# Four 32-bit transposes between the matmuls, and one transfer queue in a fixed order, in a matmul with bias and residual

## The chip, the cores and the metric

The kernel runs on one core of a Trainium2 chip. The time is device microseconds of one execution, and the median of the runs is compared. Profiles are taken of one execution by the hardware profiler; their rows are in microseconds unless marked ns. PE is TensorE's matmul, PEld its weight load, DVE is VectorE, ACT ScalarE, POOL GpSimd and SP SyncE; a q behind a name is the engine's instruction queue, from which transfers are issued.

## The reference

```python
batch, m, k, n = 16, 512, 1024, 768
x: [16, 512, 1024] f32, weight: [1024, 768] f32, bias: [768] f32, residual: [16, 512, 768] f32

def reference(x, weight, bias, residual):
    return (np.matmul(x, weight) + bias + residual).astype(np.float32)
```

## The kernel before

x is taken as 8192 rows of 1024. A tile t is 128 of these rows, so there are 64 tiles; one matmul contracts 128 of the 1024 elements of a row, so a tile has eight steps k. In DRAM the rows are cut so that each of the 128 partitions holds neighbouring rows: four rows of x in one load (16 KB in a run, `stage_xload`, L156), two rows of the residual in one load (6 KB, `stage_resload`, L163) and two rows of the result in one store (L221).

A tile goes through four stages. `stage_a` casts its rows of x to bfloat16 on ScalarE (L94). `stage_b` transposes them on TensorE, eight times 128 x 128 of bfloat16, into the PSUM tile `psum_t` (L181), and VectorE copies `psum_t` to `xt_tile` in one instruction (L96). `stage_c` does sixteen matmuls (L197): for each k, one over 512 and one over 256 of the 768 columns, with the weights of `xt_tile` held in the array and the matrix `w_sb` streamed through it. `stage_d` adds the residual to the sum on VectorE (L217), and after every second tile ScalarE's queue issues the store. The bias is added to the residual ahead of that by GpSimd (L106, a helper's line, as L94 and L96 are).

The loop over t is written so that the transposes of tile t+1 come before the matmuls of tile t, and the addition of tile t-1 after them. Its order is the program's; the framework may move an instruction where its priorities say so, and sets the waits. Loads are issued from SP's queue, as are half the weights; the other half of the weights (`W_SPLIT_ACT`), the bias and all stores are issued from ScalarE's. At most eight transfers are in flight: the issue of one waits for the end of an earlier one, on one of eight semaphores.

At the start x, the weights in single steps of k and the residual are loaded; ScalarE and VectorE cast four steps of the weights each.

The buffers: 3 of x (four tiles each), 6 of the residual, 8 of the result, 4 of cast rows, 5 of `xt_tile`, 2 of `psum_t` and 3 of the matmul's sum `psum_o`.

Of the kernel before, what the change touches and what calls it, by code (L numbers as in the profile page):

```python
# [9 lines left out]

MM_DT = mybir.dt.bfloat16
XROWS = 4
RES_ROWS = 2
STORE_ROWS = 2
X_SWDGE = False
BIAS_ENGINE = "gpsimd"
WCV_SYNC_ENGINE = "scalar"
WCV_ACT_ENGINE = "vector"
CONVERT_ENGINE = "scalar"  # L20
COPYBACK_ENGINE = "vector"
PIPE_AB = 2
XB_BUFS = 4
X_BUFS = 3
RES_BUFS = 6
OUT_BUFS = 8
XT_BUFS = 5
POUT_BUFS = 3
PTRANS_BUFS = 2
W_SPLIT_ACT = 4  # L30
K_ROTATE = 4
# [3 lines left out]
def kernel(  # L35
# [9 lines left out]
    P = 128  # L45
    FP32 = mybir.dt.float32
    BF16 = mybir.dt.bfloat16

# [4 lines left out]
    Kw, N = weight.shape  # L53
    assert Kw == K
    n_k = K // P
    n_sub = M // P
    n_xload = M // (XROWS * P)
    n_resload = M // (RES_ROWS * P)
    RES_PER_X = XROWS // RES_ROWS

    x_ld = x2d.rearrange("(S p j) k -> S p j k", p=P, j=XROWS)
    res_4d = res2d.rearrange("(S p j) n -> S p j n", p=P, j=XROWS)
    out_4d = out2d.rearrange("(S p j) n -> S p j n", p=P, j=XROWS)

    def res_ld_ap(q):
        S, h = divmod(q, RES_PER_X)
        return res_4d[S, :, h * RES_ROWS:(h + 1) * RES_ROWS, :]

    def out_st_ap(sg):
        S, h = divmod(sg, XROWS // STORE_ROWS)  # L70
        return out_4d[S, :, h * STORE_ROWS:(h + 1) * STORE_ROWS, :]

    if N <= 512:
        n_chunks = [(0, N)]
    else:
        n_chunks = [(0, 512), (512, N - 512)]

    k_order = [(K_ROTATE + i) % n_k for i in range(n_k)]

    const = ctx.enter_context(tc.tile_pool(name="const", bufs=1))  # L80
    xin_pool = ctx.enter_context(tc.tile_pool(name="xin", bufs=1))
    xbf_pool = ctx.enter_context(tc.tile_pool(name="xbf", bufs=1))
    xt_pool = ctx.enter_context(tc.tile_pool(name="xt", bufs=1))
    res_pool = ctx.enter_context(tc.tile_pool(name="res", bufs=1))
    out_pool = ctx.enter_context(tc.tile_pool(name="outp", bufs=1))
    ptrans_pool = ctx.enter_context(tc.tile_pool(name="ptrans", bufs=1, space=bass.MemoryType.PSUM))
    pout_pool = ctx.enter_context(tc.tile_pool(name="pout", bufs=1, space=bass.MemoryType.PSUM))

    def rr_tile(pool, base, idx, nbufs, shape, dtype):
        return pool.tile(shape, dtype, name=base, tag=f"{base}{idx % nbufs}", bufs=1)  # L90

    def eng_copy(eng_name, out_ap, in_ap):
        if eng_name == "scalar":
            nc.scalar.copy(out=out_ap, in_=in_ap)  # L94
        elif eng_name == "vector":
            nc.vector.tensor_copy(out=out_ap, in_=in_ap)  # L96
        elif eng_name == "gpsimd":
            nc.gpsimd.tensor_copy(out=out_ap, in_=in_ap)
        else:
            nc.any.tensor_copy(out=out_ap, in_=in_ap)  # L100

    def eng_add(eng_name, out_ap, in0, in1):
        if eng_name == "vector":
            nc.vector.tensor_add(out=out_ap, in0=in0, in1=in1)
        else:
            nc.gpsimd.tensor_add(out=out_ap, in0=in0, in1=in1)  # L106

    warm = const.tile([1, 2], FP32, name="warm")
    nc.vector.memset(warm, 0.0)  # L109
    nc.scalar.copy(out=warm, in_=warm)  # L110

    ident = const.tile([P, P], BF16, name="ident")
    make_identity(nc, ident)

    w_dram = weight.rearrange("(ko ki) n -> ki ko n", ki=P)
    w_sb = const.tile([P, n_k, N], MM_DT, name="w_sb")
    w_stage = const.tile([P, n_k, N], FP32, name="w_stage")

    with tc.high_priority():
        bias_row = const.tile([1, N], FP32, name="bias_row")  # L120
        nc.scalar.dma_start(out=bias_row, in_=bias[None, :])
        for k in range(W_SPLIT_ACT):
            nc.scalar.dma_start(out=w_stage[:, k, :], in_=w_dram[:, k, :])

    ones_col = const.tile([1, P], BF16, name="ones_col")
    nc.vector.memset(ones_col, 1.0)  # L126
    bias_row16 = const.tile([1, N], BF16, name="bias_row16")
    nc.vector.tensor_copy(out=bias_row16, in_=bias_row)  # L128
    bias_psum = pout_pool.tile([P, N], FP32, name="bias_psum", tag="psum_o0", bufs=1)
    for (n0, nl) in n_chunks:  # L130
        nc.tensor.matmul(  # L131
            bias_psum[:, n0:n0 + nl],
            lhsT=ones_col,
            rhs=bias_row16[:, n0:n0 + nl],
            start=True,
            stop=True,
        )
    bias_bcast = const.tile([P, N], FP32, name="bias_bcast")
    nc.vector.tensor_copy(out=bias_bcast, in_=bias_psum)  # L139

    x_tiles = {}
    res_tiles = {}
    out_tiles = {}
    xb_tiles = {}
    xt_tiles = {}
    psum_o_tiles = {}

    def stage_xload(sx):
        if sx >= n_xload:
            return  # L150
        if X_SWDGE:
            x_tile = rr_tile(xin_pool, "x_tile", sx, X_BUFS, [P, XROWS, K], BF16)
            nc.gpsimd.dma_start(out=x_tile, in_=x_ld[sx])
        else:
            x_tile = rr_tile(xin_pool, "x_tile", sx, X_BUFS, [P, XROWS, K], FP32)
            nc.sync.dma_start(out=x_tile, in_=x_ld[sx])  # L156
        x_tiles[sx] = x_tile

    def stage_resload(q):
        if q >= n_resload:  # L160
            return
        res_tile = rr_tile(res_pool, "res_tile", q, RES_BUFS, [P, RES_ROWS, N], FP32)
        nc.sync.dma_start(out=res_tile, in_=res_ld_ap(q))  # L163
        res_tiles[q] = res_tile
        for j in range(RES_ROWS):
            eng_add(BIAS_ENGINE, res_tile[:, j, :], res_tile[:, j, :], bias_bcast)

    def stage_a(t):
        if t < 0 or t >= n_sub:
            return  # L170
        xb_tile = rr_tile(xbf_pool, "xb_tile", t, XB_BUFS, [P, K], BF16)
        eng_copy(CONVERT_ENGINE, xb_tile, x_tiles[t // XROWS][:, t % XROWS, :])
        xb_tiles[t] = xb_tile

    def stage_b(t):
        if t < 0 or t >= n_sub:
            return
        xin = xb_tiles.pop(t)
        psum_t = rr_tile(ptrans_pool, "psum_t", t, PTRANS_BUFS, [P, n_k, P], BF16)
        for k in range(n_k):  # L180
            nc.tensor.transpose(  # L181
                out=psum_t[:, k, :],
                in_=xin[:, ts(k, P)],
                identity=ident,
            )
        xt_tile = rr_tile(xt_pool, "xt_tile", t, XT_BUFS, [P, n_k, P], MM_DT)
        eng_copy(COPYBACK_ENGINE, xt_tile, psum_t)
        xt_tiles[t] = xt_tile

    def stage_c(t):  # L190
        if t < 0 or t >= n_sub:
            return
        xt_tile = xt_tiles.pop(t)
        psum_o = rr_tile(pout_pool, "psum_o", t, POUT_BUFS, [P, N], FP32)
        for i, k in enumerate(k_order):
            for (n0, nl) in n_chunks:
                nc.tensor.matmul(  # L197
                    psum_o[:, n0:n0 + nl],
                    lhsT=xt_tile[:, k, :],
                    rhs=w_sb[:, k, n0:n0 + nl],  # L200
                    start=(i == 0),
                    stop=(i == n_k - 1),
                )
        psum_o_tiles[t] = psum_o

    def stage_d(t):
        if t < 0 or t >= n_sub:
            return
        psum_o = psum_o_tiles.pop(t)
        res_tile = res_tiles[t // RES_ROWS]  # L210
        s2, j2 = divmod(t, STORE_ROWS)
        if j2 == 0:
            out_tiles[s2] = rr_tile(
                out_pool, "out_tile", s2, OUT_BUFS, [P, STORE_ROWS, N], FP32
            )
        out_tile = out_tiles[s2]
        nc.vector.tensor_add(  # L217
            out=out_tile[:, j2, :], in0=psum_o, in1=res_tile[:, t % RES_ROWS, :]
        )
        if j2 == STORE_ROWS - 1:  # L220
            nc.scalar.dma_start(out=out_st_ap(s2), in_=out_tiles.pop(s2))  # L221
        if t % RES_ROWS == RES_ROWS - 1:
            res_tiles.pop(t // RES_ROWS)

    next_xload = [0]
    next_res = [0]

    def ensure_xloaded(sx):
        while next_xload[0] <= min(sx, n_xload - 1):
            stage_xload(next_xload[0])  # L230
            next_xload[0] += 1

    def ensure_resloaded(q):
        while next_res[0] <= min(q, n_resload - 1):
            stage_resload(next_res[0])
            next_res[0] += 1

    ensure_xloaded(0)
    for k in range(W_SPLIT_ACT, n_k):
        nc.sync.dma_start(out=w_stage[:, k, :], in_=w_dram[:, k, :])  # L240
# [47 lines left out]
```

## Time and profile before

| what | value |
|---|---|
| time, median of 3 runs | 221.37 us (221.13 to 221.74) |
| span of the profiled execution | 219.0 us |
| median of the runs less that span | 2.4 us |
| TensorE busy, matmuls and transposes | 197.0 us (90%) |
| VectorE, ScalarE, GpSimd busy | 103.5, 68.3, 114.6 us |
| bytes moved, and mean rate | 87.29 MB, 399 GB/s |
| granted TensorE clock, mean | 0.998 |

The span runs from the first to the last instruction of the profiled execution. The page does not give a time of that execution on the outside, so the difference to the median of the runs stands in the table. "Busy" for TensorE includes the modelled ends of its matmuls. In a row of the timeline the first number is the start, the second the duration from the first start to the last end of the instructions merged into it; what stands in square brackets is how long the engine had been idle, and who ended that.

### The profile page before, as it was taken

Reading aid. Unit: us, or ns where it says so; the run is one execution under the profiler, and the core shown is the slowest. Engines: PE = TensorE matmul, PEld = TensorE weight load, DVE = VectorE, ACT = ScalarE, POOL = GpSimd, SP = SyncE. Lnnn points to the kernel's source line nnn. Section 1 sums busy time; section 2 is a strip of 40 time slices with the busy share of each in tenths; the row PEclk is TensorE's granted clock in tenths of the full one; section 3 lists DMA queues with packets and bytes.
Section 4 is the critical chain, followed back from the end, with each engine's and each line's share of the span. In section 5 each row is a group of like instructions: output and inputs, shape, how many; then the busy total and the mean of one; then the engine's idle time right before and its main releaser. Section 6 shows DMA issues by size and latency. Waiting matters only on the chain.

```text
span 219.0 us, 3761 instructions
## 1 busy us (share of the span) xinstructions
PE 197.0 (90%) x1509; PEld 130.3 (60%) x1538; DVE 103.5 (47%) x136; ACT 68.3 (31%) x70; POOL 114.6 (52%) x70
## 2 busy tenths in 40 slices
PE   1119989999999999999999999999999999999990
PEld 0115656666666666666666666666666666666660
DVE  1133454455544555445554455444554445544441
ACT  2362243352240706051420607051331607042000
POOL 1006751919275573909284663919184482918900
PEclk9999999999999999999999999999999999999999
DMA  7999999999999999999999999999999999999433
GB/s 235 399 409 440 428 404 441 413 424 439 412 436 412 434 413 433 428 422 430 419 435 416 441 409 435 428 420 432 413 434 414 444 405 436 427 413 398 188 144 144
DMA packets 12692, 87.29 MB, mean 399 GB/s; under 512 B 1409, under 2 KB 1409, under 8 KB 10626
## 3 DMA queue, kind: packets, MB, share of 16 engines
q1 hardware_dynamic: 7488, 60.30, 65.7%
q10 hardware_dynamic: 5186, 26.74, 29.5%
q8 instruction: 12, 0.20, 0.4%
q14 instruction: 6, 0.05, 0.1%
HBM read 61.87 MB, written 25.17 MB: 397 GB/s over the span
## 4 chain that ended last, share of the span: by engine, by line
PE 82%; issue 1%; DVE 0%; DVEq 0%
PE psum_o L197 71%; PE psum_t L181 12%; DVE out_tile L217 0%; DVEq L217 0%
## 5 line engine op out<-in xcount | busy, mean ns | idle before, releaser
L197 PE MATMUL psum_o<-w_sb,xt_tile 128*128 128x256 bf16 (+1 forms) x995 | 175.5, 326 | 7.5 <-DVE xt_tile L96 6.0
L106 POOL TENSOR_TENSOR res_tile<-res_tile,bias_bcast 128x768 f32<-128x768 f32 x64 | 113.9, 1813 | 93.1 <-DMA res_tile<-in_residual_dram 87.5
L197 PEld LDWEIGHTS <-xt_tile 128*128 128x128 bf16 x1024 | 97.8, 98 | 65.0 <-DVE xt_tile L96 6.2
L217 DVE TENSOR_TENSOR out_tile<-psum_o,res_tile 128x768 f32<-128x768 f32 x64 | 61.3, 957 | 96.7 <-PE psum_o L197 51.0
L94 ACT CAST xb_tile<-x_tile 128x1024 bf16<-128x1024 f32 x64 | 63.7, 1042 | 124.8 <-DMA x_tile<-in_x_dram 69.4
L181 PE MATMUL psum_t<-ident,xb_tile 128*128 128x128 bf16 x512 | 40.1, 223 | 6.5 <-ACT xb_tile L94 6.5
L96 DVE COPY xt_tile<-psum_t 128x1024 bf16<-128x1024 bf16 x64 | 43.4, 680 | 2.2 <-PE psum_t L181 2.2
L181 PEld LDWEIGHTS <-xb_tile 128*128 128x128 bf16 x512 | 34.8, 100 | 15.4 <-ACT xb_tile L94 7.3
L96 DVE CAST w_sb<-w_stage 128x768 bf16<-128x768 f32 x4 | 2.2, 560 | 10.5 <-DMA w_stage<-in_weight_dram 10.5
L94 ACT CAST w_sb<-w_stage 128x768 bf16<-128x768 f32 x4 | 3.3, 832 | 1.9 <-DMA w_stage<-in_weight_dram 1.9
L131 PE MATMUL bias_psum<-bias_row_97,ones_col 1*128 1x512 bf16 (+1 forms) x2 | 0.8, 498 | 2.7 <-DVE bias_row_97 L128 2.7
L110 ACT ACT_TABLE_LOAD x1 | 1.3, 1283 | 3.5 <-issue 3.5
L131 PEld LDWEIGHTS <-ones_col 1*128 1x128 bf16 x2 | 0.2, 99 | 2.6 <-issue 1.6
L128 DVE CAST bias_row_97<-bias_row 1x768 bf16<-1x768 f32 x1 | 0.5, 547 | 1.1 <-DMA bias_row<-in_bias_dram 1.1
L139 DVE COPY bias_bcast<-bias_psum 128x768 f32<-128x768 f32 x1 | 0.9, 950 | 0.0
L109 DVE MEMSET warm<- 1x2 f32 x1 | 0.1, 60 | 0.8 <-PEq L272 0.8
masks.py:197 POOL MEMSET ident<- 128x128 bf16 x1 | 0.2, 205 | 0.3 <-POOLq L272 0.3
masks.py:199 POOL TENSOR_SCALAR_AFFINE_SELECT ident<-ident 128x128 bf16<-128x128 bf16 x1 | 0.3, 293 | 0.1
L272 POOL MEMSET const-float32-0.0<- 128x1 f32 x1 | 0.1, 99 | 0.2 <-issue 0.2
L110 ACT COPY warm<-warm 1x2 f32<-1x2 f32 x1 | 0.2, 191 | 0.0
L126 DVE MEMSET ones_col<- 1x128 bf16 x1 | 0.2, 165 | 0.0
L272 POOL MEMSET const-bfloat16-1.0<- 128x1 bf16 x1 | 0.1, 103 | 0.0
(2 smaller groups left out, 0.2 us busy)
## 6 DMA issues: line engine op xcount, KB each, us to landing
x_tile<-in_x_dram SPq DMA_DIRECT2D x16, 2048.0 KB, 21.1
res_tile<-in_residual_dram SPq DMA_DIRECT2D x32, 768.0 KB, 19.1
out_dram<-out_tile ACTq DMA_DIRECT2D x32, 768.0 KB, 10.7
w_stage<-in_weight_dram SPq DMA_DIRECT2D x4, 384.0 KB, 9.7
w_stage<-in_weight_dram ACTq DMA_DIRECT2D x4, 384.0 KB, 10.9
bias_row<-in_bias_dram ACTq DMA_DIRECT2D x1, 3.0 KB
```

Of the source, the lines that this page charges most:

```text
L94: nc.scalar.copy(out=out_ap, in_=in_ap)
L96: nc.vector.tensor_copy(out=out_ap, in_=in_ap)
L106: nc.gpsimd.tensor_add(out=out_ap, in0=in0, in1=in1)
L110: nc.scalar.copy(out=warm, in_=warm)
L126: nc.vector.memset(ones_col, 1.0)
L128: nc.vector.tensor_copy(out=bias_row16, in_=bias_row)
L131: nc.tensor.matmul(bias_psum[:, n0:n0 + nl], lhsT=ones_col, rhs=bias_row16[:, n0:n0 + nl], start=True, stop=True,)
L139: nc.vector.tensor_copy(out=bias_bcast, in_=bias_psum)
L181: nc.tensor.transpose(out=psum_t[:, k, :], in_=xin[:, ts(k, P)], identity=ident,)
L197: nc.tensor.matmul(psum_o[:, n0:n0 + nl], lhsT=xt_tile[:, k, :], rhs=w_sb[:, k, n0:n0 + nl], start=(i == 0), stop=(i == n_k - 1),)
L217: nc.vector.tensor_add(out=out_tile[:, j2, :], in0=psum_o, in1=res_tile[:, t % RES_ROWS, :])
L272: nc = _bacc.Bacc("TRN2", target_bir_lowering=False, num_devices=1)
```

## The change

The kernel is written anew around the same arithmetic. In short:

- A row of x is still cast to bfloat16 on ScalarE, but it is transposed as 512 words of 32 bits, each of two neighbours. A tile takes four transposes in place of eight (`transpose`). A transposed word has two steps of the contraction in it, so the matmul takes every second element of `xt` as weights (`lhsT=xt_tiles[t][:, c, :, r]`), and the weight matrix is loaded with its rows paired in the same way (`w_dram`).
- The four transposes of tile t+1 stand between the matmuls of tile t, one behind the 512-wide matmul of k = 0, 2, 4 and 6. The copy out of PSUM remains one instruction for each tile.
- All transfers but the bias are issued from SP's queue in a written order, and the framework keeps the program's order on each engine (`tc.keep_in_program_order`). The residual is loaded, and the result stored, four rows to a partition (12 KB in a run). The last group is stored row by row. The first group of x is loaded row by row, between the weights.
- The first three tiles advance together through the steps of k as the weights come. All weights are cast on VectorE. 24 matmuls on the identity run on TensorE ahead of them, and the bias is broadcast by a matmul of float32.
- The result of the first three groups of four tiles is made in tiles of its own: VectorE adds the bias, GpSimd then the residual. From the fourth group on the bias is added by GpSimd to the residual ahead of time, three tiles before use, and VectorE adds the sum in place, where the store reads it. Residual, result and staged weights share a ring of nine buffers.
- There are 4 buffers of x, 4 of cast rows, 3 of `xt`, 2 of the transposes' PSUM and 3 of the matmuls'.

The diff removes the old body of the function; the new core is this.

```diff
+G = 4
+X_BUFS = 4
+RING = 9
+XB_BUFS = 4
+XT_BUFS = 3
+PT_BUFS = 2
+PO_BUFS = 3
+LATE = 3
+FIRST = 3
+WARM = 24
...
+    w_dram = weight.rearrange("(c p r) n -> p c r n", p=P, r=2)
...
+    def transpose(t, c):
+        if t >= n_sub:
+            return
+        if c == 0:
+            pt_tiles[t] = slot(pt_pool, "pt", PT_BUFS, [P, n_c, P], FP32)
+        xw = xb_tiles[t].bitcast(FP32)
+        o(nc.tensor.transpose(out=pt_tiles[t][:, c, :], in_=xw[:, ts(c, P)], identity=ident))
...
+    def copy_xt(t):
+        if t >= n_sub:
+            return
+        xt_tiles[t] = slot(xt_pool, "xt", XT_BUFS, [P, n_c, P, 2], BF16)
+        o(nc.vector.tensor_copy(out=xt_tiles[t].rearrange("p c m r -> p (c m r)"),
+                                in_=pt_tiles.pop(t).rearrange("p c m -> p (c m)").bitcast(BF16)))
...
+    def matmul(t, k0=0, k1=n_k, ahead=None):
...
+        for k in range(k0, k1):
+            c, r = divmod(k, 2)
+            for (n0, nl) in chunks:
+                o(nc.tensor.matmul(
+                    po_tiles[t][:, n0:n0 + nl],
+                    lhsT=xt_tiles[t][:, c, :, r],
+                    rhs=w_sb[:, c, r, n0:n0 + nl],
+                    start=(k == 0),
+                    stop=(k == n_k - 1),
+                ))
+
+                if ahead is not None and n0 == 0 and r == 0:
+                    transpose(ahead, c)
+
+    def evacuate(t):
...
+        if g < LATE:
...
+            o(nc.vector.tensor_add(out=ot[:, j, :], in0=po, in1=bias_bc))
+            o(nc.gpsimd.tensor_add(out=ot[:, j, :], in0=ot[:, j, :], in1=r_tiles[g][:, j, :]))
         else:
...
+            o(nc.vector.tensor_add(out=rt[:, j, :], in0=po, in1=rt[:, j, :]))
...
+    load_x(0, 0, 1)
+    load_w(0)
+    load_x(0, 1, 2)
+    load_w(1)
+    load_x(0, 2, 3)
+    load_w(2)
+    load_w(3)
+    load_x(0, 3, 4)
+    load_x(1, 0, 2)
+    load_x(1, 2, 4)
+    load_x(2)
+    load_r(0)
+    load_x(3)
+    load_r(1)
+    load_r(2)
+    load_r(3)
...
+    for i in range(WARM):
+        o(nc.tensor.matmul(warm_ps, lhsT=warm_in, rhs=warm_in, start=True, stop=True))
...
+    matmul(2, 0, 4)
+    cast_w(4)
+    cast_w(5)
+    for t in range(FIRST):
+        matmul(t, 4, 6)
+    cast_x(3)
+    cast_w(6)
+    cast_w(7)
+    for t in range(FIRST):
+        matmul(t, 6, 8)
+    for c in range(n_c):
+        transpose(3, c)
+    copy_xt(3)
+    cast_x(4)
+    cast_x(5)
+    for t in range(FIRST):
+        evacuate(t)
+
+
+    for t in range(FIRST, n_sub):
+        g, j = divmod(t, G)
+        cast_x(t + 3)
+        matmul(t, ahead=t + 1)
+        copy_xt(t + 1)
+        evacuate(t)
+        add_bias(t + 3)
+        if j == G - 1:
+            if g + 4 < n_grp:
+                load_x(g + 4)
+            if g < n_grp - 1:
+                store(g)
+            if g + 4 < n_grp:
+                load_r(g + 4)
+        if g == n_grp - 1:
+            store(g, j, j + 1)
```

## The prediction

> **What bounds the kernel now.** First the page's head, slices and chain, to see which engine sets the end and whether the transfers could.
>
> ```profile
> span 219.0 us, 3761 instructions
> PE 197.0 (90%) x1509; PEld 130.3 (60%) x1538; DVE 103.5 (47%) x136; ACT 68.3 (31%) x70; POOL 114.6 (52%) x70
> ...
> DMA  7999999999999999999999999999999999999433
> ...
> PE 82%; issue 1%; DVE 0%; DVEq 0%
> PE psum_o L197 71%; PE psum_t L181 12%; DVE out_tile L217 0%; DVEq L217 0%
> ```
>
> TensorE is the chain that ends last, and the transfers are close behind: the DMA row reads 9 from the second slice until the loads run out some 17 us before the end. Both bounds need a price. The tile's rhythm comes from the timeline, TensorE and VectorE between 98.9 and 105 us.
>
> ```profile
> 98.69 2.76 PE L197 MATMUL psum_o<-w_sb,xt_tile 128*128 128x512 bf16 x16
> 101.29 0.61 PE L181 MATMUL psum_t<-ident,xb_tile 128*128 128x128 bf16 x8
> 101.73 2.76 PE L197 MATMUL psum_o<-w_sb,xt_tile 128*128 128x512 bf16 x15
> 104.33 0.61 PE L181 MATMUL psum_t<-ident,xb_tile 128*128 128x128 bf16 x8
> ...
> 101.54 0.96 DVE L217 TENSOR_TENSOR out_tile<-psum_o,res_tile 128x768 f32<-128x768 f32 x1 [1.48 <-issue]
> 102.42 0.68 DVE L96 COPY xt_tile<-psum_t 128x1024 bf16<-128x1024 bf16 x1
> ```
>
> A tile takes 3.05 us: sixteen matmuls from 101.73 to 104.33 (2.60) and eight transposes in 0.45, 0.056 each. Single rows of the trace give a start-to-start time of 0.216 for a 512-wide matmul, 0.109 for a 256-wide one. All transposes of tile t+1 stand ahead of the matmuls of tile t, so the 0.68 us copy has 2.60 us of matmuls to hide under. Thus the copy costs nothing today. The waits of TensorE say the same: it waited for xt_tile 6.0 us in all, in two places, both before 32 us.
>
> Next, the links from transpose to copy and from copy to matmul, where nothing else held the waiting engine, and the end of the kernel.
>
> ```profile
> 18.63 1.06 PE L181 MATMUL psum_t<-ident,xb_tile 128*128 128x128 bf16 x8
> ...
> 19.73 0.69 DVE L96 COPY xt_tile<-psum_t 128x1024 bf16<-128x1024 bf16 x1 [2.24 <-PE psum_t L181]
> ...
> 30.91 1.28 DVE L96 COPY xt_tile<-psum_t 128x1024 bf16<-128x1024 bf16 x2
> ...
> 31.65 2.39 PEld L197 LDWEIGHTS <-xt_tile 128*128 128x128 bf16 x16 [0.99 <-DVE xt_tile L96]
> ```
>
> The eight transposes end at 19.69 and the copy starts at 19.73: 0.04. After the last matmul, 213.46 + 0.273 = 213.73, the last addition starts at 213.84: 0.11. I take 0.07. The first of the two copies at 30.91 ends at 31.59 and the weight load starts at 31.65: 0.06. A transpose ends 0.219 after its start (the tile view of psum_t, median).
>
> **The change on TensorE.** In the new steady loop (`matmul(t, ahead=t+1)`) the four transposes follow the 512-wide matmuls of k = 0, 2, 4 and 6. `copy_xt(t + 1)` is still one copy of the whole tile, so it waits for the fourth; the instruction listing has the first weight load of tile t+1 wait for VectorE, right behind tile t's last matmul. Take a four-byte transpose at the two-byte one's 0.056 first. The fourth starts after six pairs (6 x 0.325 = 1.95), a 512-wide matmul (0.216) and three transposes (0.168): 2.33 us into the tile. From there 0.219 + 0.07 + 0.68 + 0.06 = 1.03 until the next tile may start, so a tile takes 3.36 us. Behind that transpose TensorE has only 0.109 + 0.216 + 0.109 of matmuls to do: some 0.54 us per tile it stands still, where the transposes saved give back 4 x 0.056 = 0.22. Net +0.31. This is the decisive step: cover for the copy is cut from sixteen matmuls to three.
>
> The price of a four-byte transpose isn't in the trace. Lower bound: 0.056, same width. Upper: 0.216, the 512-wide row, as though words went through in four passes. Between: 0.109, the 256-wide row, which streams as many bytes. I take 0.056, since rows of equal width cost equal time here, and its weight load has the 0.216 of the matmul before it to hide in. [...] The matmuls' weights are now read with a step of two elements; contiguous loads have 98 ns rows at a pitch of 0.056 in the transposes. Doubled, they would still fit under 0.109, and cost 0.05 only behind each transpose: the 0.109 case again.
>
> **Start.** Packet records of the trace: 611 ns for 16,384 bytes, 234 for 6,144, 121 for 3,072, which is 8 ns and 27.2 bytes per ns. One queue moves x row 0, w, x row 1, w and so on, eight packets per engine each: 1.28 us for a row of x (estimate from the fit), 1.88 for two k of w, starting at 1.75. Weights are complete at 13.4, row 2 of x at 9.6. Tile 2's matmuls can start at 14.1 (its transposes queue behind those of tiles 0 and 1). From there 5.2 us (1.3 + twice 1.95) of matmuls, transposes of tile 3 to 19.5, copy to 20.5, and addition 0 (0.96), which frees the PSUM buffer and stands behind that copy on VectorE: the loop starts at 21.4, where tile 3 starts at 27.2 now. That is 5.8 us gained, if the 24 warm-up matmuls hold the faster pitch: transposes stand 0.107 apart at 19 us and 0.056 at 24 us now; at the slow pitch the start costs 5 more.
>
> **Transfers.** Bytes stay. Packets of 12,288 bytes (460 ns by the fit) take the place of two of 6,144: 8 ns times 3,968 over 16 engines, 2.0 us less. All told 204.4 us for each engine by the fit, 205 to 206 as the trace exceeds its medians by 1%. A group of four tiles needs 5.24 MB, 12.3 us, against 4 x 3.36 = 13.4 of TensorE: covered, with 8% in hand. Stores now stand in SP's queue. `store(g)` waits for the group's last addition, and behind it are the loads of r and x four groups on; with eight transfers in flight (each issue waits for the eighth before it, as now) nothing needs them for three groups. Without that cover, each group would wait a store's 3.7 us.
>
> **At nothing.** ACT loses the 32 store issues and four w casts (68.3 us busy, idle 124.8 before x casts); POOL keeps 64 additions of 1.81 (115 of 230 us); VectorE gets four more w casts at 0.56, in the start above, and per tile 0.68 + 0.96 of 3.36. The three groups whose residual POOL adds after the matmul are stored later, early on when the queue is full.
>
> **Sum.** 21.4, plus 60 tiles x 3.36 = 201.8 until tile 63 starts, 2.60 for it, 0.27 to the addition, 0.96 for it. From there to the end it is 4.16 now (214.80 to 218.96); a store of one row, 3,072-byte packets for 6,144, saves 8 x 0.113 = 0.9: 3.26. Span 230.3. The median 221.37 is 2.41 above the span of 218.96, and I add that: 232.7 us, 11.3 more than now. (About 0.3% is what a measurement can tell from no change here.)
>
> **Rivals.** *Copy covered, transfers the bound (faster).* If from the fourth transpose to the next tile's first matmul is 0.75 us or less, a tile falls under the 12.3/4 = 3.08 us that transfers need, and the time is theirs: 1.75 + 205.5 + about 1.3 to the end, 208.6, with 2.4: 211. For it: DMA rows at 9, and the smaller sum on TensorE, 2.60 + 0.22 = 2.82. Against: copies last 678 to 691 ns in 64 of 64, so the chain would have to lose 0.28 of links of which 0.06 and 0.04 are the waits. Between lies little: 3.2 us per tile breaks even.
>
> *Step or words at the 256-wide price.* At 0.109: 2.17 + 0.33 + 0.27 + 0.07 + 0.68 + 0.06 = 3.58; with a start of 22.3, 243.9 + 2.4 = 246.
>
> *Weight load uncovered, or four passes.* At 0.163 (0.056 plus one 256-wide slot, nearest to a load that waits) a tile is some 3.80 and the time 261; at 0.216, 4.00 and 273. For: no row shows four-byte operands. Against: weight loads here start ahead, with the matmul before.
>
> *The words don't work as one transpose of two:* excluded by the listing, four transposes per tile and a copy of the same 1024 elements.
>
> **Numbers.** Forecast, 226 to 240: 0.52 (low end 3.33 us per tile with the short links and a start two earlier; high end a slow start, or 0.07 per transpose). The 246 case, 240 to 252: 0.20. Uncovered or four passes: 0.13, two thirds of it under 262. Faster, near 211: 0.14. Within 0.3%: 0.01. Range 226 to 262, which leaves out the 0.15 below and the 273 case.
>
> **What the new profile would show.** Right: TensorE idle before xt some 0.5 us in each tile, 30 us in all, released by VectorE's copy; transposes at 0.056; tiles 3.36 apart from 21.4 on; DMA slices below 9 in the second half, and SP waiting for VectorE before stores. Wrong: weight loads of xt that wait under 0.2; the DMA row at 9 to the end (first rival); transposes over 0.1 apart from the matmul behind them (the others).

## The result and the profile after

The changed kernel takes 248.54 us (median of 4 runs, 246.26 to 248.63); the kernel before took 221.31 beside it. The ratio is 1.12 (95% interval 1.1154 to 1.1247). The forecast was 232.7 us in a range of 226 to 262: the direction was right, the loss was 27.2 us in place of 11.3, and the time is nearest to that of the second rival, 246 us. In all that follows, medians and ranges are of all runs of a kernel, and a ratio leaves out a run over 1.5% above its kernel's fastest (one run each of the copy in halves and of the order k = 0, 2, 4, 5).

The page of the changed kernel, head, DMA slices and the chain that ended last:

```profile
span 246.9 us, 3277 instructions
PE 214.6 (87%) x1308; PEld 139.1 (56%) x1308; DVE 104.6 (42%) x139; ACT 68.3 (28%) x66; POOL 114.7 (46%) x70
...
DMA  6999999999999999999999999999999633060623
...
PE 77%; DVE 19%; issue 2%; DMA 1%; DVEq 0%
PE po L146 62%; DVE xt L137 18%; PE pt L129 12%; PE bias_ps L198 1%; PE warm_ps L204 1%; DMA bias_row<-in_bias_dram 1%; DVE o_tile L165 0%; DVE r_tile L169 0%; DVE w_sb L121 0%; DVEq L169 0%
```

VectorE, which had 0% of the chain before, has 19% now, and 18% of the span is one line: the copy from `pt` to `xt` (L137). The page counts the modelled end of each matmul as busy, so PE at 87% hides the idle time; the waits show it (engine, line, releaser: us in total, times, longest):

```profile
PEld L146 <- DVE xt L137: 46.3, 62, 1.2
...
PE po L146 <- DVE xt L137: 22.6, 62, 0.8
```

For every tile of the loop but its first, and for two ahead of it, TensorE waits for the copy: in the loop 0.74 us ahead of the first weight load and 0.35 us ahead of the first matmul. One tile on the timeline, TensorE and VectorE:

```profile
111.33 0.39 PE L146 MATMUL po<-w_sb,xt 128*128 128x512 bf16 x1 [0.35 <-DVE xt L137]
...
111.56 0.27 PE L129 MATMUL pt<-ident,xb 128*128 128x128 f32 x1
...
111.67 0.81 PE L146 MATMUL po<-w_sb,xt 128*128 128x256 bf16 x4
...
113.84 0.27 PE L129 MATMUL pt<-ident,xb 128*128 128x128 f32 x1
...
113.95 0.60 PE L146 MATMUL po<-w_sb,xt 128*128 128x256 bf16 x3
114.15 0.69 DVE L137 COPY xt<-pt 128x1024 bf16<-128x1024 bf16 x1 [2.01 <-PE pt L129]
...
114.90 0.39 PE L146 MATMUL po<-w_sb,xt 128*128 128x512 bf16 x1 [0.35 <-DVE xt L137]
```

The fourth transpose starts at 113.84, 2.51 us into the tile. The copy starts 0.31 later, takes 0.69, and the next tile starts at 114.90: a chain of 1.06 us, beside which TensorE has three matmuls. Tiles are 3.56 us apart, 0.52 more than the 3.04 that TensorE's own work takes. A transpose occupies TensorE for 0.11 us, from 111.56 to the matmul at 111.67; from rows before rounding it is 0.109.

Against the profile before, tile 3 starts at 25.83 for 27.2 (1.4 gained), the sixty tiles until tile 63 take 213.8 us for 183.8 (30.0 lost), and from tile 63's start to the end it is 7.3 for 8.0 (0.7 gained). Together 27.9 are lost, the difference of the spans.

### The profile page after: what moved, and what is told of

The parts are those of the page before. It is cut to its first block, busy times and chain, and to the rows that moved or that the text cites. A ratio compares the mean times of both kernels' runs of the same rounds, so it can differ in the third digit from the quotient of the medians.

```text
span 246.9 us, 3277 instructions
## 1 busy us (share of the span) xinstructions
PE 214.6 (87%) x1308; PEld 139.1 (56%) x1308; DVE 104.6 (42%) x139; ACT 68.3 (28%) x66; POOL 114.7 (46%) x70
## 4 chain that ended last, share of the span: by engine, by line
PE 77%; DVE 19%; issue 2%; DMA 1%; DVEq 0%
PE po L146 62%; DVE xt L137 18%; PE pt L129 12%; PE bias_ps L198 1%; PE warm_ps L204 1%; DMA bias_row<-in_bias_dram 1%; DVE o_tile L165 0%; DVE r_tile L169 0%; DVE w_sb L121 0%; DVEq L169 0%
## 5 line engine op out<-in xcount | busy, mean ns | idle before, releaser
L146 PE MATMUL po<-w_sb,xt 128*128 128x512 bf16 (+1 forms) x1024 | 206.3, 330 | 25.5 <-DVE xt L137 22.6
L146 PEld LDWEIGHTS <-xt 128*128 128x128 bf16 x1024 | 100.4, 98 | 96.3 <-DVE xt L137 46.3
L175 POOL TENSOR_TENSOR r_tile<-r_tile,bias_bc 128x768 f32<-128x768 f32 x52 | 92.7, 1817 | 55.0 <-DMA r_tile<-in_residual_dram 44.2
L117 ACT CAST xb<-x_tile 128x1024 bf16<-128x1024 f32 x64 | 66.8, 1046 | 156.1 <-PE pt L129 142.5
L137 DVE COPY xt<-pt 128x1024 bf16<-128x1024 bf16 x64 | 44.2, 691 | 131.6 <-PE pt L129 131.6
L129 PE MATMUL pt<-ident,xb 128*128 128x128 f32 x256 | 69.0, 278 | 0.0
L169 DVE TENSOR_TENSOR r_tile<-po,r_tile 128x768 f32<-128x768 f32 x52 | 49.2, 947 | 2.3 <-PE po L146 2.1
L129 PEld LDWEIGHTS pt<-ident,xb 128*128 128x128 f32 x256 | 36.6, 144 | 2.7 <-issue 0.6
L166 POOL TENSOR_TENSOR o_tile<-o_tile,r_tile 128x768 f32<-128x768 f32 x12 | 21.5, 1810 | 34.3 <-DMA r_tile<-in_residual_dram 31.5
L165 DVE TENSOR_TENSOR o_tile<-po,bias_bc 128x768 f32<-128x768 f32 x12 | 11.2, 947 | 0.0
## 6 DMA issues: line engine op xcount, KB each, us to landing
r_tile<-in_residual_dram SPq DMA_DIRECT2D x16, 1536.0 KB, 20.7
```

Source lines behind the costliest of these rows:

```text
L117: o(nc.scalar.copy(out=xb_tiles[t], in_=x_tiles[t // G][:, t % G, :]))
L129: o(nc.tensor.transpose(out=pt_tiles[t][:, c, :], in_=xw[:, ts(c, P)], identity=ident))
L137: o(nc.vector.tensor_copy(out=xt_tiles[t].rearrange("p c m r -> p (c m r)"), in_=pt_tiles.pop(t).rearrange("p c m -> p (c m)").bitcast(BF16)))
L146: o(nc.tensor.matmul(po_tiles[t][:, n0:n0 + nl], lhsT=xt_tiles[t][:, c, :, r], rhs=w_sb[:, c, r, n0:n0 + nl], start=(k == 0), stop=(k == n ...
L165: o(nc.vector.tensor_add(out=ot[:, j, :], in0=po, in1=bias_bc))
L166: o(nc.gpsimd.tensor_add(out=ot[:, j, :], in0=ot[:, j, :], in1=r_tiles[g][:, j, :]))
```

## The experiments

The theory: the time is lost because the copy's cover was cut to three matmuls. Then a tile takes the larger of two numbers, TensorE's own 2.60 + 4 x 0.109 = 3.04 us, and the start of the last transpose in the tile plus the chain of 1.06. The rivals: the four-byte words or their strided weights cost the time, or the single queue and the start do.

**The four transposes behind k = 0, 1, 2, 3.**

```diff
-                if ahead is not None and n0 == 0 and r == 0:
-                    transpose(ahead, c)
+                if ahead is not None and n0 == 0 and k < n_c:
+                    transpose(ahead, k)
```

> The four transposes of tile t+1 stand behind the 512-wide matmuls of k = 0, 1, 2, 3 in place of 0, 2, 4, 6; nothing else changes. If the lost cover is the cause: the last transpose starts 1.52 us into the tile (3 x 0.325 + 0.216 + 3 x 0.109), the next tile could start 0.27 + 0.04 + 0.69 + 0.06 later, at 2.58, before its matmuls end at 2.60 + 0.44 = 3.04. TensorE's wait for xt goes from 0.74 at the weight load to nothing, the tile from 3.56 to 3.04, and as transfers need 3.08 the two bounds meet: 217 to 220 us. If the single queue or its order holds the kernel up (rival), nothing is won: 244 to 249. If weight loads can't run ahead of a four-byte transpose (rival), the tile stays above 3.2: over 226.

Measured: 216.91 us (214.06 to 217.19), ratio to the kernel before 0.9757 (0.9693 to 0.9822). From its timeline and its waits:

```profile
113.85 0.27 PE L129 MATMUL pt<-ident,xb 128*128 128x128 f32 x1
...
115.15 0.27 PE L129 MATMUL pt<-ident,xb 128*128 128x128 f32 x1
...
115.26 1.79 PE L146 MATMUL po<-w_sb,xt 128*128 128x256 bf16 x10
...
115.46 0.69 DVE L137 COPY xt<-pt 128x1024 bf16<-128x1024 bf16 x1 [0.60 <-PE pt L129]
...
116.89 0.27 PE L129 MATMUL pt<-ident,xb 128*128 128x128 f32 x1
```

```profile
PE po L146 <- DVE xt L137: 1.6, 2, 0.8
```

The time is just under its forecast. The copy of 115.46 to 116.15 now lies under ten matmuls. Tiles are 3.04 us apart, and the wait for `xt` falls from 22.6 us in 62 places to 1.6 in two, both ahead of the loop. Nothing but the place of the transposes differs, so their place carries all of the loss: 31.6 us, more than the 27.2 between the two kernels.

**Eight two-byte transposes at the places of the four.** Contiguous weights again, two transposes behind each of k = 0, 2, 4, 6.

```diff
-        o(nc.tensor.transpose(out=pt_tiles[t][:, c, :], in_=xw[:, ts(c, P)], identity=ident))
+        for k in (2 * c, 2 * c + 1):
+            o(nc.tensor.transpose(out=pt_tiles[t][:, k, :], in_=xb_tiles[t][:, ts(k, P)], identity=ident))
...
-                    lhsT=xt_tiles[t][:, c, :, r],
+                    lhsT=xt_tiles[t][:, k, :],
```

> The changed kernel with eight two-byte transposes a tile, two at each of the same four places, contiguous weights and the weight rows in their old order. If a four-byte transpose costs what two two-byte ones cost (0.109 against 2 x 0.056), the words give nothing and take nothing: tile 3.57, 247 to 250 us. If the words and the stepped weight reads are what makes the tile long (rival), it falls to 3.4 or less: 238 or under. If words did save half of the transposes' time (rival), this kernel is slower: 260.

Measured: 249.29 us (249.2 to 249.81), ratio 1.1254 (1.1221 to 1.1287), tile 3.57. Timeline:

```profile
113.37 0.28 PE L129 MATMUL pt<-ident,xb 128*128 128x128 bf16 x2
...
115.19 0.39 PE L145 MATMUL po<-w_sb,xt 128*128 128x512 bf16 x1 [0.35 <-DVE xt L137]
```

Two-byte transposes leave the same 0.35 us of wait, and the same time within 0.3%. So the words, as against eight two-byte transposes, are not the cause.

**Contiguous weights, words kept.** The matmul takes 128 neighbouring elements of `xt` in place of every second one, and so contracts other elements than the reference.

```diff
-                    lhsT=xt_tiles[t][:, c, :, r],
+                    lhsT=xt_tiles[t].rearrange("p c m r -> p c (m r)")[:, c, ts(r, P)],
```

> The matmuls read 128 contiguous elements of xt as weights in place of every second one, so the products are of the wrong elements; instructions and sizes are the same. If the slot of 0.109 is the four-byte transpose itself: no change, tile 3.56, 248 us. If it is the stepped weight load right behind it (rival): slot 0.056, tile 3.36, about 236 us.

Measured: 247.24 us (245.74 to 248.83), ratio 1.1156 (1.1081 to 1.1231). Timeline:

```profile
113.00 0.27 PE L129 MATMUL pt<-ident,xb 128*128 128x128 f32 x1
...
113.11 0.81 PE L146 MATMUL po<-w_sb,xt 128*128 128x256 bf16 x4
```

The transpose still holds 0.109 and the tile 3.56. The step of two elements in the weights costs the tile nothing; the 0.109 belongs to the four-byte transpose itself.

**The kernel before with the words alone.** Four transposes in one block ahead of the matmuls, as its eight were.

```diff
-        psum_t = rr_tile(ptrans_pool, "psum_t", t, PTRANS_BUFS, [P, n_k, P], BF16)
-        for k in range(n_k):
+        psum_t = rr_tile(ptrans_pool, "psum_t", t, PTRANS_BUFS, [P, n_k // 2, P], FP32)
+        for k in range(n_k // 2):
...
-                in_=xin[:, ts(k, P)],
+                in_=xin.bitcast(FP32)[:, ts(k, P)],
...
-                    lhsT=xt_tile[:, k, :],
+                    lhsT=xt_tile[:, k // 2, :, k % 2],
```

> The kernel before with the words alone: four four-byte transposes a tile in one block ahead of the matmuls, stepped weights, weight rows paired. By the slot of 0.109: 0.44 a tile in place of 0.45, the copy still covered: 219.5 to 221.5 us, no difference to speak of. If four-byte weight loads (rows of 140 ns) show where no 512-wide matmul covers them (rival): 0.14 each, 0.11 more a tile, 228 us.

Measured: 220.19 us (220.17 to 220.73), ratio 0.9937 (0.9916 to 0.9959). Timeline:

```profile
113.45 0.60 PE L181 MATMUL psum_t<-ident,xb_tile 128*128 128x128 f32 x4
...
113.88 2.76 PE L198 MATMUL psum_o<-w_sb,xt_tile 128*128 128x512 bf16 x16
```

From 113.45 to 113.88 four words take 0.43 us, against 0.44 for the eight of before (101.29 to 101.73). Half the instructions at twice the price: the words give a tile nothing, and the slower weight loads of four-byte words (144 ns in the changed kernel, where the two-byte transposes of before have 100) cost nothing here either, where no 512-wide matmul lies between them: the four of this block run from 113.34 to 113.81, and the transposes take 0.11 each. The kernel takes 1.6 us (0.6%) less all the same; the sixty tiles, at 3.063 and 3.054 us on average, account for 0.5 of it, and the rest I did not follow.

**Transposes behind k = 0, 2, 4, 5, and behind k = 1, 3, 5, 7.** These move the last transpose by one step of k each way, which tests the sum for the tile at two more points.

```diff
-                if ahead is not None and n0 == 0 and r == 0:
-                    transpose(ahead, c)
+                if ahead is not None and n0 == 0 and k in (0, 2, 4, 5):
+                    transpose(ahead, (0, 2, 4, 5).index(k))
```

```diff
-                if ahead is not None and n0 == 0 and r == 0:
+                if ahead is not None and n0 == 0 and r == 1:
```

> The changed kernel with its transposes behind k = 0, 2, 4, 5. By the sum: the last starts at 5 x 0.325 + 0.216 + 3 x 0.109 = 2.17, and 1.08 later the next tile: 3.25 in place of 3.56, 60 x 0.31 = 18.7 less: 229 to 231 us. If it were the mere count of interruptions or the four-byte words (rival): no change.

> The changed kernel with its transposes behind k = 1, 3, 5, 7. By the sum: the last starts at 7 x 0.325 + 0.216 + 3 x 0.109 = 2.82, the next tile 1.08 later: 3.90 in place of 3.56, 60 x 0.33 = 19.8 more: 267 to 270 us. If it were the mere count of interruptions or the four-byte words (rival): no change.

Measured: 226.73 us (225.84 to 230.05), ratio 1.0227 (1.0185 to 1.0268); and 265.21 us (265.0 to 266.8), ratio 1.1993 (1.1955 to 1.2031). Timeline of the second:

```profile
115.29 0.27 PE L146 MATMUL po<-w_sb,xt 128*128 128x256 bf16 x1
...
116.24 0.71 PE L146 MATMUL po<-w_sb,xt 128*128 128x512 bf16 x3 [0.68 <-DVE xt L137]
```

One 256-wide matmul is left behind the fourth transpose, and the wait grows to 0.68. The sum, with 0.325 for a pair of matmuls, 0.216 for the 512-wide one, 0.109 for a transpose and 1.06 for the chain:

| last transpose behind | its start | + 1.06 | tile by the sum | tile measured |
|---|---|---|---|---|
| k = 3 | 1.52 | 2.58 | 3.04 (TensorE's own) | 3.037 |
| k = 5 | 2.17 | 3.23 | 3.23 | 3.239 |
| k = 6 (the change) | 2.49 | 3.55 | 3.55 | 3.563 |
| k = 7 | 2.82 | 3.88 | 3.88 | 3.888 |

The chain of 1.06 comes from the changed kernel, and the same sum holds at the three other places. Both times are below their forecasts, which had counted on the change's start. The profiled execution of the second had tile 3 at 22.92, 2.9 us before the change's; that of the first was its longest run, 230.05, with tile 3 at 26.7, and its three other runs (225.84 to 227.54) are shorter by 2.5 to 4.2 us.

**The copy in two halves, transposes where the change has them.** The first half goes behind the second transpose, the second behind the fourth.

```diff
-        o(nc.vector.tensor_copy(out=xt_tiles[t].rearrange("p c m r -> p (c m r)"),
-                                in_=pt_tiles.pop(t).rearrange("p c m -> p (c m)").bitcast(BF16)))
+        o(nc.vector.tensor_copy(out=xt_tiles[t][:, h:h + 2].rearrange("p c m r -> p (c m r)"),
+                                in_=pt[:, h:h + 2].rearrange("p c m -> p (c m)").bitcast(BF16)))
...
                     transpose(ahead, c)
+                    if c == 1:
+                        copy_half(ahead, 0)
```

> The changed kernel with its transposes where they are, at k = 0, 2, 4, 6, but the copy cut in two: the first half of xt behind the second transpose, the second half behind the fourth. Steps k = 0 to 3 of the next tile need the first half only. If the exposed copy is the cause: TensorE has no wait between tiles (the second half is ready 0.78 after the fourth transpose starts, at 3.27 us, and is needed at 4.34), tile 3.04, 216 to 219 us. If the place of the transposes costs TensorE something of its own (rival): the tile stays at 3.2 or more, 226 or over.

Measured: 220.64 us (219.15 to 222.83, 10 runs), ratio 0.9947 (0.9914 to 0.998). Timeline and waits:

```profile
116.48 0.14 PEld L129 LDWEIGHTS pt<-ident,xb 128*128 128x128 f32 x1 [0.26 <-DVE xt L145]
```

```profile
PEld pt L129 <- DVE xt L145: 15.6, 60, 0.5
```

With half of the chain's copy (0.42 us) behind the last transpose, and the first matmuls needing only the first half, the tile is 3.13 us. That misses the forecast of 3.04 and 216 to 219 us, but lies below the 3.2 of the rival. So most of the loss comes back from the copy's side too, at unchanged places on TensorE. The 0.09 above 3.04 is a new wait: the next tile's first transpose stands behind the second half's copy. By the program it writes the other PSUM buffer and doesn't need that copy; why it waits was not settled.

**The early order, with filling in the start.** 10, 6 and 6 matmuls on the identity follow the transposes of tiles 0, 1 and 2.

```diff
+FILL = (10, 6, 6)
...
+    def fill(n, ps):
+        for i in range(n):
+            o(nc.tensor.matmul(ps, lhsT=warm_in, rhs=warm_in, start=True, stop=True))
```

> The kernel with the transposes behind k = 0 to 3, and 22 more matmuls on the identity in the start, where TensorE waits for the first copies of x: 10, 6 and 6 behind the transposes of tiles 0, 1, 2. In the profile of the change the clock record has half the clock until 17.2 us, in the run with contiguous weights until 8.2, and there tile 3 started 2.9 us earlier (22.96 against 25.83). If that is what the late start lacked: full clock before 12 us, tile 3 at 23 to 24, 214 to 215.5 us, and a narrower spread. If the arrival of x and the weights sets the start (rival): tile 3 at 25.5 or later, 217 us.

Measured: 214.17 us (214.06 to 214.94), ratio 0.9673 (0.9648 to 0.9699). Tile 3 starts at 22.82, where the early order without filling had 25.56 in its profiled execution. Without filling three runs read 216.8 to 217.2 and one 214.06; with it all four lie within 0.9 us of that one. In the traces' clock records full clock starts at 8.4 us here, and at 10.7 and 7.8 in the two kernels below with the same filling; in the nine profiled kernels that have the new start without it, between 8.2 and 18.2. The filling fits this, but with one profiled execution for each kernel it isn't shown to be the reason.

**The early order, addition 0 ahead of tile 3's copy.**

```diff
+    evacuate(0)
     copy_xt(3)
...
-    for t in range(FIRST):
+    for t in range(1, FIRST):
```

> The kernel with the transposes behind k = 0 to 3, and the addition of tile 0 put ahead of the copy of tile 3 on VectorE. TensorE waits 1.65 us for that addition before tile 3, as it frees the PSUM buffer. If TensorE's chain alone sets the end: tile 3 starts 0.9 earlier, 216 us. If the transfers do (rival): no change.

Measured: 216.26 us (214.81 to 217.22), ratio 0.9754 (0.9709 to 0.98); tile 3 at 25.27 for 25.56. The addition is off TensorE's path: it ends 0.14 us before the four transposes that the copy needs, and from these to tile 3 it is 1.38 us in place of 2.25, the 0.9 that was forecast. But the transposes start 0.6 later than in the early order's profile, in an execution whose full clock came at 17.8 us for 16.6, and 0.3 is left at tile 3. For the time it is inconclusive: the medians differ by less than the spread of these runs.

**Early order, filled, and tile 3 prepared behind tile 0's last matmuls.**

```diff
-    for t in range(FIRST):
-        matmul(t, 6, 8)
+    matmul(0, 6, 8)
     for c in range(n_c):
         transpose(3, c)
+    evacuate(0)
     copy_xt(3)
+    for t in range(1, FIRST):
+        matmul(t, 6, 8)
```

> The kernel with early transposes and the filled start, and tile 3 prepared sooner: its transposes, the addition of tile 0 and its copy come behind tile 0's last matmuls, with those of tiles 1 and 2 (1.3 us) as cover. Tile 3 starts at 22.82 now; TensorE's chain alone would give 20.7 and 212 us. If the transfers are as close behind as the DMA row says (9 to 205 of 212 us), less comes of it: 212.5 to 214. Rival: x for the next tiles isn't there, so the tiles behind wait and nothing is won, 214 to 215.

Measured: 213.02 us (212.98 to 213.09), ratio 0.9621 (0.9607 to 0.9636), tile 3 at 21.41. It beats both kernels. The page shows its transfers at 9 up to the last two slices, at 97.8% of the span of 211.2 us.

```profile
DMA  6999999999999999999999999999999999999984
...
q1 hardware_dynamic: 8496, 87.04, 97.8%
```

That the transfers keep it from 212 isn't shown: tile 3 came 0.7 us later than the 20.7 of TensorE's chain, and of the 1.4 that it gained, 0.3 is lost again at one tile near 61 us, where VectorE had waited for GpSimd. The sixty tiles take 182.5 us, 3.04 each.

**The early order, stores from ScalarE's queue.**

```diff
-        o(nc.sync.dma_start(out=o_g[g, :, j0:j1, :], in_=src[:, j0:j1, :]))
+        o(nc.scalar.dma_start(out=o_g[g, :, j0:j1, :], in_=src[:, j0:j1, :]))
```

> The kernel with the transposes behind k = 0 to 3, and all stores issued from ScalarE's queue, as before the change, in place of SP's. SP waits 125 us ahead of stores, with loads behind them in its queue. If those loads are needed three groups later only: no difference, 216 to 218 us. If the waits starve the transfers (rival): the loads come sooner, and the time falls by 1 us or more. If casts behind the stores on ScalarE come late (rival): slower, above 219.

Measured: 223.98 us (223.25 to 224.46), ratio 1.0106 (1.0077 to 1.0134): 7.1 us more than with the stores on SP. Waits and timeline:

```profile
PEld pt L129 <- ACT xb L117: 8.4, 1, 8.4
```

```profile
31.80 7.07 POOL L166 TENSOR_TENSOR o_tile<-o_tile,r_tile 128x768 f32<-128x768 f32 x4 [30.50 <-DMA r_tile<-in_residual_dram]
...
39.38 3.88 ACT L117 CAST xb<-x_tile 128x1024 bf16<-128x1024 f32 x4 [15.72 <-POOL o_tile L166]
```

It is one stall. Store 0 waits on ScalarE for GpSimd's additions, which wait for the residual and end at 38.87; four casts are queued behind the store, and TensorE stands 8.4 us for `xb`. While it stands the granted clock falls (0.60 from 36 to 39 us, 0.50 from 39 to 42), and the rows behind the stall are slower until it is back: a transpose stands 0.21 us ahead of the matmul behind it from 41.39 to 43.31, and 0.11 again at 45.00. That one tile takes 12.72 us, 9.7 more than the others; tile 3 came 2.6 earlier than in the early order's profile (22.95 for 25.56), which leaves the 7.1. So the stores on SP's queue are not a cost of this change: moving them to ScalarE's is.

**Early order, filled, residual and result two rows to a transfer.**

```diff
-        o(nc.sync.dma_start(out=r_tiles[g], in_=r_g[g]))
+        for j in (0, 2):
+            o(nc.sync.dma_start(out=r_tiles[g][:, j:j + 2, :], in_=r_g[g, :, j:j + 2, :]))
```

> The kernel with early transposes and the filled start, residual loads and stores cut to two rows a transfer, 6,144-byte packets in place of 12,288. By 8 ns a packet the transfers take 2.0 us more over 16 engines. If they bind as much as TensorE does here: 215 to 216.5. If TensorE alone binds: no change, 214. Rival: half as many bytes in the eight transfers in flight let the queue run dry at stores: 217 or more.

Measured: 218.24 us (216.57 to 219.02), ratio 0.9847 (0.9802 to 0.9891), 4.1 us more than with four rows. A DMA engine's packets took 212.6 us for 207.5. The prediction's 8 ns for each of 3,968 extra packets on 16 engines account for 2.0 of it; the rest was not taken apart. Here the transfers set the end, not TensorE: in the profiled execution, 4.9 us longer than that with four rows, tile 63 starts 1.1 us later (206.11 for 205.03), and the other 3.9 lie behind that start (11.1 us to the end for 7.25), where SP waits 5.8 us for the last stores to land (2.0 with four rows). The time is in the range of the rival, 217 or more, but whether the queue ran dry at stores wasn't tested.

## Why the prediction went right and wrong

**Right: the mechanism.** The copy's cover, not the words, the weights' step or the queue, sets the tile, and it cuts as the prediction's decisive step said. The chain from the fourth transpose's start to the next tile was put at 1.03 and measured 1.06 (0.31 to the copy for 0.29, 0.69 for 0.68, 0.06 for 0.06). VectorE's 19% of the chain and its 62 waits are what it asked for. Transfers bound nothing with 3.56 us per tile, as it said, though the DMA row stays at 9 until slice 31 and not only in the first half: the loads ran ahead until they ran out. SP's waits for results before its stores are there too (163.5 us for `r_tile`, 35.4 for `o_tile`), and nothing on TensorE's path waits for them in the loop.

**Wrong: the price of the four-byte transpose.** The prediction took 0.056 "since rows of equal width cost equal time here", and kept 0.109, the 256-wide row "which streams as many bytes", for its second rival at 0.20. The second was the price: its sign, over 0.1 between a transpose and the matmul behind it, is what the profile shows. The transpose of 128 columns of four-byte words takes 0.109 us, as a matmul over 256 two-byte columns does. The three transposes ahead of the last add 3 x 0.053 = 0.16 us to its start, and with the 0.03 of the chain and roundings the tile is 3.563 for 3.363: 60 x 0.20 = 12.0 us of the miss. The rival's own sum was 3.58; its time of 246 us, 2.6 below the measured one, has two errors that partly cancel, tile 3 at 22.3, which is 3.5 early, and the tile 0.02 too long, which is 1.0 in sixty.

The prediction also weighed a price of the weight load. The four-byte ones measure 144 ns where two-byte ones have 98:

```profile
L129 PEld LDWEIGHTS pt<-ident,xb 128*128 128x128 f32 x256 | 36.6, 144 | 2.7 <-issue 0.6
```

They lie under the 512-wide matmul ahead (one from 113.62 to 113.76, its transpose at 113.84) and cost nothing, and in the block of four transposes nothing either: a transpose takes 0.11 in both. So the third rival, which had 0.163 or 0.216, fell.

**Wrong: the start.** Tile 3 was put at 21.4 and came at 25.83. Two things were off. First, the clock: the prediction let the 24 warm-up matmuls bring the full pitch, with 5 us as the price if not. The start of the changed kernel, profiled execution:

```profile
5.02 2.74 PE L204 MATMUL warm_ps<-ident 128*128 128x128 bf16 x24
...
12.96 4.02 PE L146 MATMUL po<-w_sb,xt 128*128 128x512 bf16 x12 [0.79 <-DVE xt L137]
...
25.83 0.39 PE L146 MATMUL po<-w_sb,xt 128*128 128x512 bf16 x1 [1.65 <-DVE o_tile L165]
```

and of the kernel with contiguous weights, whose start has the same instructions:

```profile
12.15 2.12 PE L146 MATMUL po<-w_sb,xt 128*128 128x512 bf16 x12 [0.79 <-DVE xt L137]
...
15.50 5.37 PE L146 MATMUL po<-w_sb,xt 128*128 128x512 bf16 x32 [0.79 <-DVE xt L137]
...
22.96 0.39 PE L146 MATMUL po<-w_sb,xt 128*128 128x512 bf16 x1 [1.65 <-DVE o_tile L165]
```

The same twelve matmuls take 4.02 us in one execution and 2.12 in the other. The time from row to row falls to half at 17.2 us in the first (from 0.213 to 0.113 between transposes) and at 8.2 in the second, each time within a block of four transposes. The traces' clock records have their first entry, full clock, at the same moments; the page's PEclk row reads 9 throughout and doesn't show it. The earlier onset gives 25.83 - 22.96 = 2.9 of the 4.4 us.

Second, what stands ahead of tile 2. Even in the execution with the early clock its matmuls start at 15.50, for the 14.1 of the prediction: 1.4 of the remaining 1.5 us. The prediction worked from the arrivals of x and of the weights, with tile 2's transposes behind those of tiles 0 and 1. Its 14.1 doesn't follow from the terms that it gives, and its 9.6 and 13.4 are 0.3 above their own sums (1.75 + 3 x 1.28 + 2 x 1.88 = 9.35, and 13.1 with the other weights). The chain that ended last starts elsewhere, here in the execution with the early clock:

```profile
0.73 1.82 DMA bias_row<-in_bias_dram
2.68 2.90 PE bias_ps L198 x4
5.58 2.67 PE warm_ps L204 x24
```

The transposes of tile 0 stand behind the bias' matmul and the warm-up and start at 8.04, though the cast that they need was done at 6.13; the prediction's sum has neither of the two. The data of row 2 does come later than reckoned: its cast starts at 11.94 in place of 9.6. But that cast is done at 12.98, 1.1 us before TensorE is through with the twelve matmuls ahead, so it delays nothing. What the start would be without the two was not run.

For one order of instructions, then, the onset came 9.0 us apart (17.2 and 8.2). That the filled start's four times lie within 0.9 us of each other fits an early onset in each; what sets the moment, no run shows.

**The rest.** From tile 63's start to the end it was 7.3 us, where the prediction had 7.1. The profiled execution took 248.63, 1.8 more than its span, for 2.4. Sum of the miss: 12.0 + 4.4 + 0.2 - 0.6 = 16.0, which to rounding is 248.6 - 232.7 = 15.9.

**The first rival** (copy covered, transfers the bound, 211 us) was wrong for this change, where the copy isn't covered. Once it is, the best version comes to 213.02, near the rival's time. But the 3.08 us that the transfers were said to need is no floor for a single tile: the early order's sixty tiles take 3.037 each with no wait among them, and the transfers have the start and the end of the kernel besides.

## What to carry to other kernels

When an operation is spread between others, what counts is what its consumer's chain still has beside it: take the start of the last piece, add the chain to the next user, and compare with the work left (here 1.06 us against 0.43 of matmuls; behind k = 3 it is covered, behind k = 6 it costs 0.52 per tile). Don't price an operation of a wider type by the row with as many columns: the four-byte transpose cost the 0.109 us of the row with as many bytes, not the 0.056 of the one with as many columns. Bytes are no general rule either. In the start of the changed kernel, at half the pace, the float32 matmul of the bias over 512 columns has two records: from the first start to the second it is 0.99 us, and from the second to the next instruction 0.85, 1.84 in all, where a 512-wide bfloat16 matmul at that pace takes 0.43. That is over four times the time for twice the bytes, so such a price is best measured. And before a store is put on an engine's queue, ask what is queued behind it there.

## What the runs showed of the hardware

- A transpose of 128 x 128 four-byte words holds TensorE for 0.109 us at full clock, twice the two-byte one's 0.056, so two neighbours per word save instructions and no time (0.43 us for four, 0.44 for eight).
- For one order of instructions the full TensorE clock came at 8.2 us in one execution and at 17.2 in another, worth 2.9 us; with 22 small matmuls in the gaps of the start it came at 8.4, 10.7 and 7.8 in three profiled kernels, and the four runs of the first agree within 0.9 us.
- While TensorE stood 8.4 us early in the loop, with the stores on ScalarE's queue, its granted clock fell to 0.50, and that tile took 9.7 us more than the others.
- Half-size transfers for residual and result cost 4.1 us, twice the 2.0 us that 8 ns for each of the 3,968 extra packets account for, the fixed part by the fit to the packet records of before (611 ns for 16,384 bytes, 234 for 6,144, 121 for 3,072).
